# Differential scores: a copying minimum in place of a bare one, and an exponential on chip memory

## The chip, the core and the metric

The kernel runs on one NeuronCore of one Trainium2 chip. The core's engines run side by side, each through its own list of instructions in order: TensorE (PE; its weight loads are shown as PEld), VectorE (DVE), ScalarE (ACT), GpSimd (POOL) and SyncE (SP), which here only issues transfers. [...] The metric is the device time of one execution in microseconds (us); lower is better.

## What is computed

One layer of a bidirectional encoder over 1040 tokens (1024 plus 16 meta tokens) of width 1024: a SwiGLU block, a mixing block whose heads are split between differential attention and windowed attention, and a second SwiGLU block. The change lies in the differential attention, 4 heads with two score maps each:

```python
def attend(qb):
    s = jnp.einsum('bqhcd,bkhcd->bhcqk', qb, k, preferred_element_type=jnp.float32) * scale
    p = jax.nn.softmax(s, axis=-1)
    a = p[:, :, 0] - lam * p[:, :, 1]
    return jnp.einsum('bhqk,bkhe->bqhe', a.astype(v.dtype), v)
```

Each of the two maps c = 0, 1 of a head is a softmax over all 1040 keys; the second is weighted with a learned number and subtracted from the first, and the difference multiplies the values.

## The kernel before

The queries are handled in units of 128 rows, 8 units to a head, 32 in all; below, "unit 16" is the first one of the third head, and its two maps are 16a (c = 0) and 16b (c = 1). `scores` handles one map of one unit: six matmuls (three column ranges, with the keys split into a high and a low part) write the negated scores into a PSUM tile `ds` of 1040 columns, DVE reduces it to the row minimum `dmx`, and ACT takes the exponential out of PSUM into the SBUF tile `dp`, with the row sum as a second result. The tile `ds` spans three of the eight PSUM banks and there is one for each c (rings `ds0` and `ds1`, one slot each; the first three units use `ds0` for both), so the matmuls of the next unit's map must wait until the last reader of this one's `ds` is through. The two remaining banks are one slot `dt` for transposes and one slot `do` for products.

`combine` then makes the difference: DVE takes the reciprocals `drz` of the row sums (L797), POOL scales the second map (L799), DVE adds the first one to it (L800). Two units later PE transposes the result in three pieces through the slot `dt` (L1173 twice, L1181), each copied to `at` by ACT (L1178, L1182) or DVE (L1176), and every second unit the transposed rows multiply the values (L1189). Between these, PE works through products of the output projection with the windowed heads (L167 there). Loads of the next head's keys and queries pass through ACT (`kh` at L117, `qst` at L765) and POOL.

The tiles `dp` have three slots for each c, `dmx` two. The program is written as generators that take turns, but the framework's scheduler settles each engine's final order from its own timing model, over the whole program.

The window attention ahead of it already contains the instruction that the change uses, with a mask as its second input:

```python
nc.vector.tensor_tensor_reduce(
    out=p4[:, g, :w], in0=ps[:, :w], in1=mk[:, :w], scale=1.0,
    scalar=nsink[:, hh : hh + 1], op0=ALU.add, op1=ALU.min, accum_out=mx[:, g : g + 1],
)
```

Of the kernel before, what the change touches and what calls it, by code (L numbers as in the profile page):

```python
# [10 lines left out]
F32 = mybir.dt.float32  # L11
F32R = mybir.dt.float32r
AF = mybir.ActivationFunctionType
ALU = mybir.AluOpType
AX = mybir.AxisListType
# [3 lines left out]
P = 128  # L19
# [4 lines left out]
L = SEQ + NM  # L24
# [27 lines left out]
def layer(  # L52
# [4 lines left out]
    nc = tc.nc  # L57

    def mk_pool(name, bufs=1, side="left", space=None):
        kw = {"space": space} if space is not None else {}  # L60
        return tc.tile_pool(name=name, bufs=bufs, reuse_waits="tile", side=side, **kw)
# [21 lines left out]
    cpool = ctx.enter_context(mk_pool("cpool"))  # L83
# [9 lines left out]
    gains = const("gains", [P, 4, KT])  # L93
    eps = cpool.tile([P, 1], F32, name="eps")
    nc.vector.memset(eps, EPS)
    warm = cpool.tile([P, 1], F32, name="warm")
    nc.scalar.activation(warm, eps, AF.Abs_reciprocal_sqrt)
    nc.vector.tensor_scalar(gains, gains, -0.5 / D, None, op0=ALU.mult)
# [83 lines left out]
    def chunk_aps(ps, chunks):  # L182
        off = OFF if chunks is CH_ALL else 0
        return [ps[:, off + c0 : off + c0 + n] for c0, n in chunks], ps[
            :, off : off + chunks[-1][0] + chunks[-1][1]
        ]
# [592 lines left out]
    def scores(head, qt, c, tiles, ds):  # L779
        khs, kls, qs = head[:3]  # L780
        ps_p, z = tiles
        ps = ds.tile([P, 1536], F32, tag="ds", name="ds")
        outs, full = chunk_aps(ps, CH_ALL)
        for i, kk in enumerate((khs[c], kls[c])):
            for o, (c0, n) in zip(outs, CH_ALL):
                nc.tensor.matmul(
                    o, qs[c][:, qt * P : (qt + 1) * P], kk[:, c0 : c0 + n], start=i == 0, stop=i == 1
                )
        mx = dp.tile([P, 1], F32, tag=f"dmx{c}", name=f"dmx{c}")
        nc.vector.tensor_reduce(mx, full, axis=AX.X, op=ALU.min)  # L790
        p = dp.tile([P, L], F32, tag=f"dp{c}", name=f"dp{c}", bufs=3)
        nc.scalar.activation(p, full, AF.Exp, bias=mx, scale=-1.0, accum_out=z[:, c : c + 1])
        ps_p.append(p)

    def combine(ps_p, z):
# [9 lines left out]
    with ExitStack() as st:  # L805
# [236 lines left out]
        for i, (kv, n) in enumerate(units):  # L1042
            if i + 1 < len(units):
                keys[i + 1] = win_keys(*units[i + 1])
            p4 = win_scores(kv, n, [qs[kv, g] for g in range(4)], keys.pop(i))
            if prev:
                win_values(*prev)
            if i == 13:
                for _ in fill:
                    pass  # L1050
                st_u.close()
                kp = Rings(st_k, "kp", "right")
                for tag, bufs in (("v", 2), ("qst", 3), ("kh", 3), ("kl", 3), ("kraw", 1), ("qraw", 1)):
                    kp.reserve(tag, bufs)
                dp = Rings(st_k, "dp", "right", bufs=2)
                for tag, bufs in (("dp0", 3), ("dp1", 3), ("at", 2), ("oh", 2)):
                    dp.reserve(tag, bufs)
                ds0 = Rings(st_k, "ds0", "right", space=PSUM).reserve("ds")
                heads[0] = load_head(0)
            prev = (kv, n, p4)  # L1060
            if i in EARLY:
                for t in EARLY[i]:
                    sc[t] = score_tiles()
                    for c in range(2):
                        scores(heads[0], t, c, sc[t], ds0)
                    pend[t] = combine(*sc.pop(t))
            if n == NB - 1 and kv == 0:
                for g in range(4):
                    qs[1, g] = win_q(4 + g)
# [9 lines left out]
    with ExitStack() as st:  # L1079
        op = Rings(st, "op").reserve("ow_hi").reserve("ow_lo")  # L1080
# [123 lines left out]
        for i in range(NQ + 4):  # L1204
# [3 lines left out]
            def do_scores(c):  # L1208
                if N_EARLY <= i < NQ:
                    scores(heads[i // NB], i % NB, c, sc[i], ds1 if c else ds0)  # L1210
# [40 lines left out]
            if i >= 7 and (i - 7) % 4 == 0:  # L1251
                hd2, c = divmod((i - 7) // 4, 2)
# [168 lines left out]
```

## Time and profile before

| | |
|---|---|
| time, median of 3 runs | 2092.57 us (2092.17 to 2096.58) |
| profiled execution, its own time | 2091.47 us |
| its span, first to last instruction | 2089.7 us |
| PE busy | 1956.9 us (94%) |
| DVE busy | 1262.0 us (60%) |
| POOL busy | 993.3 us (48%) |
| ACT busy | 882.8 us (42%) |
| mean granted PE clock | 0.973 of full speed |

The busy times are shares of the whole span; what a stage can gain is read from the waits inside it. A busy PE is not PE at its peak, since matmuls overlap and their ends are modelled.

### The profile page before, as it was taken

The page shows a single profiled execution, that of the slowest core. Times are in us where ns is not written, and L with a number is a line of the kernel's source. Part 1 is how long each engine was busy: PE and PEld are TensorE (multiplying, and loading weights), DVE is VectorE, ACT ScalarE, POOL GpSimd, SP SyncE. Part 2 cuts the span into 40 slices and gives each one's busy share as a digit, 9 for nine tenths or more (in the row PEclk, how much of TensorE's full clock was granted, in tenths as well). Part 3 has the DMA queues.
Part 4 walks back from the last instruction along what each step waited for, and adds up shares of the span by engine and source line. Part 5 has one row for each costly group of instructions (what it writes and reads, how often), then busy time and mean ns, then how long its engine had stood idle before and what let it go on. Part 6 is the DMA issues. An engine that isn't in the chain of part 4 may idle for free. (4 is left out here: it accounts for less than half of the span.)

```text
span 2089.7 us, 30414 instructions
## 1 busy us (share of the span) xinstructions
PE 1956.9 (94%) x11508; PEld 1701.2 (81%) x11508; DVE 1262.0 (60%) x1843; ACT 882.8 (42%) x1611; POOL 993.3 (48%) x811
## 2 busy tenths in 40 slices
PE   6999999998999989899978898897999999989998
PEld 5999999998999879778756677675788888867877
DVE  6755555548874661276668677466655455487745
ACT  6433333334432431366566666353333333344433
POOL 0555554545443740576446442017754554454543
PEclk8999999999999999999979999998999999999999
DMA  4332322328422351544443321522333233385122
GB/s 157 110 118 97 117 91 99 108 94 314 153 62 81 130 165 62 152 118 121 109 102 91 83 75 53 194 92 81 122 106 111 86 106 112 116 297 166 61 81 81
DMA packets 106002, 244.14 MB, mean 117 GB/s; under 512 B 14208, under 2 KB 29008, under 8 KB 105856
## 3 DMA queue, kind: packets, MB, share of 16 engines
q1 hardware_dynamic: 94336, 204.53, 30.9%
q0 software_dynamic: 11520, 37.67, 4.6%
q8 instruction: 90, 1.47, 0.3%
q14 instruction: 56, 0.46, 0.1%
HBM read 169.86 MB, written 65.44 MB: 113 GB/s over the span
## 5 line engine op out<-in xcount | busy, mean ns | idle before, releaser
L226 PE MATMUL p<-t_hi,wch 128*128 128x260 f32 (+1 forms) x528 | 142.9, 325 | 9.4 <-DVE u L114 9.4
L226 PE MATMUL p<-b_hi,wah 128*128 128x260 f32 (+1 forms) x528 | 144.4, 328 | 7.0 <-ACT b_hi L117 3.8
L226 PE MATMUL p<-b_hi,wal 128*128 128x260 f32 (+1 forms) x528 | 142.3, 325 | 6.4 <-DVE wal L114 6.4
L226 PE MATMUL p<-b_lo,wah 128*128 128x260 f32 (+1 forms) x528 | 143.7, 325 | 0.0
L226 PE MATMUL p<-t_lo,wch 128*128 128x260 f32 (+1 forms) x528 | 142.2, 324 | 0.0
L226 PE MATMUL p<-t_hi,wcl 128*128 128x260 f32 (+1 forms) x528 | 141.9, 323 | 0.0
L114 DVE TENSOR_TENSOR u<-p,m 128x520 f32<-128x520 f32 (+1 forms) x88 | 61.0, 693 | 129.2 <-PE p L226 129.1
L114 POOL TENSOR_TENSOR ru<-rg,ru 128x512 f32<-128x512 f32 x44 | 87.6, 1990 | 106.8 <-DVE hb L149 74.0
L226 PE MATMUL p<-t_hi,wbh 128*128 128x260 f32 (+1 forms) x504 | 133.7, 321 | 2.6 <-ACT wbh L117 2.6
L226 PE MATMUL p<-t_lo,wbh 128*128 128x260 f32 (+1 forms) x504 | 135.9, 320 | 0.0
L226 PE MATMUL p<-t_hi,wbl 128*128 128x260 f32 (+1 forms) x504 | 133.3, 320 | 0.0
L117 ACT CAST wch<-ru 128x512 fp32r<-128x512 f32 x88 | 54.8, 623 | 183.8 <-issue 89.5
L574 PE MATMUL pA<-bh,wh 128*128 128x260 f32 (+1 forms) x432 | 116.3, 323 | 5.4 <-DVE h L581 5.4
L117 ACT CAST wbh<-s 128x512 fp32r<-128x512 f32 x84 | 52.3, 622 | 152.1 <-PE p L226 137.3
L574 PE MATMUL pA<-bl,wh 128*128 128x260 f32 (+1 forms) x432 | 115.5, 321 | 0.0
L114 POOL TENSOR_TENSOR s<-ru 128x512 f32<-128x512 f32 x42 | 57.4, 1368 | 120.3 <-DMA ru<-wu 60.9
L574 PE MATMUL pA<-bh,wl 128*128 128x260 f32 (+1 forms) x432 | 112.3, 319 | 0.0
L114 DVE TENSOR_TENSOR bl<-r,bh 128x520 fp32r<-128x520 f32 (+1 forms) x126 | 109.9, 907 | 2.3 <-ACT bh L117 2.0
L114 POOL TENSOR_TENSOR s<-wr 128x384 f32<-128x384 f32 x48 | 55.2, 1153 | 114.0 <-DVE wl L114 94.2
L117 ACT CAST wh<-s 128x384 fp32r<-128x384 f32 x96 | 49.1, 515 | 136.8 <-PE pA L574 66.6
L581 DVE SCALAR_TENSOR_TENSOR h<-pA,h 128x520 f32<-128x520 f32 (+1 forms) x96 | 66.2, 691 | 63.1 <-PE pA L574 63.0
L117 ACT CAST wah<-rg 128x512 fp32r<-128x512 f32 x88 | 54.4, 621 | 117.9 <-PE p L226 89.2
(289 smaller groups left out, 6128.0 us busy)
## 6 DMA issues: line engine op xcount, KB each, us to landing
rg<-wg SPq DMA_DIRECT2D x44, 512.0 KB, 3.6
ru<-wu SPq DMA_DIRECT2D x44, 512.0 KB, 5.2
wr<-wd SPq DMA_DIRECT2D x24, 768.0 KB, 4.4
r<-g_t SPq DMA_DIRECT2D x12, 780.0 KB, 5.9
r<-g_t SPq DMA_DIRECT2D x12, 768.0 KB, 5.8
g_b<-g POOLq DMA_DIRECT2D x27, 260.0 KB, 5.2
r<-g_b SPq DMA_DIRECT2D x9, 780.0 KB, 4.9
g_b<-g POOLq DMA_DIRECT2D x27, 256.0 KB, 5.5
```

The lines of the kernel that those rows point to most:

```text
L114: eng.tensor_tensor(out, a, b, op=op)
L117: nc.scalar.copy(hi, src)
L226: nc.tensor.matmul(o, w_k(ww, k), x[:, k, c0 : c0 + cn], start=first and k == 0 and i == 0, stop=k == hk - 1 and i == 2, skip_group_check= ...
L574: nc.tensor.matmul(o, w_k(ww, k), xx[:, c0 : c0 + cn], start=new and k == 0 and q == 0, stop=k == DNG - 1 and q == 2, skip_group_check=not ...
L581: nc.vector.scalar_tensor_tensor(hs, full, 0.5, hs, op0=ALU.mult, op1=ALU.add)
```

## The change

The row minimum is no longer a reduction that only reads. One DVE instruction adds zero to the scores, writes the sum (the scores themselves) to `dp` in SBUF, and leaves the row minimum in `dmx`; the zeros are a column `zero` of one element per partition, read with a stride of 0. The exponential then reads `dp` and writes `dp`. The slot of `dp` is taken by the DVE instruction now, not by ACT.

```diff
     nc.vector.memset(eps, EPS)
+    zero = cpool.tile([P, 1], F32, name="zero")
+    nc.vector.memset(zero, 0.0)
...
         mx = dp.tile([P, 1], F32, tag=f"dmx{c}", name=f"dmx{c}")
-        nc.vector.tensor_reduce(mx, full, axis=AX.X, op=ALU.min)
         p = dp.tile([P, L], F32, tag=f"dp{c}", name=f"dp{c}", bufs=3)
-        nc.scalar.activation(p, full, AF.Exp, bias=mx, scale=-1.0, accum_out=z[:, c : c + 1])
+        nc.vector.tensor_tensor_reduce(
+            out=p, in0=full, in1=zero.broadcast_to([P, L]), scale=1.0, scalar=3.4028234663852886e38,
+            op0=ALU.add, op1=ALU.min, accum_out=mx,
+        )
+        nc.scalar.activation(p, p, AF.Exp, bias=mx, scale=-1.0, accum_out=z[:, c : c + 1])
         ps_p.append(p)
```

The scheduler orders the whole program anew. Three places show what that does; a name in square brackets is the engine whose progress the instruction waits for (Pool is POOL, Activation is ACT, DMAHW a transfer), and line numbers of the changed kernel stand 2 to 5 higher. All three are at units 16 and 17, the first of the third head.

On DVE, before:

```order
L790 TENSOR_REDUCE dmx0_13802<-ds_13795 128x1 [waits PE_49]
L1176 COPY at_13674<-dt_13769 128x4x128 [waits PE_49]
L800 SCALAR_TENSOR_TENSOR dp0_13737<-dp0_13737,drz_13817,dp1_13748 128x1040 [waits Pool_49]
L790 TENSOR_REDUCE dmx1_13813<-ds_13806 128x1 [waits PE_49]
L1176 COPY at_13794<-dt_13821 128x4x128 [waits PE_49]
```

and in the changed kernel:

```order
L793 ISA dp1_13816,dmx1_13815<-ds_13808,zero_68 128x1040 [waits PE_49]
L793 ISA dmx1_13815 128x1
L1181 COPY at_13676<-dt_13771 128x4x128 [waits PE_49]
L805 SCALAR_TENSOR_TENSOR dp0_13738<-dp0_13738,drz_13819,dp1_13749 128x1040 [waits Pool_49]
L793 ISA dp1_13869,dmx1_13868<-ds_13861,zero_68 128x1040 [waits PE_49]
L793 ISA dmx1_13868 128x1
L793 ISA dp0_13805,dmx0_13804<-ds_13797,zero_68 128x1040 [waits PE_49]
L793 ISA dmx0_13804 128x1
```

Each reduction has become a pair, the pass over 1040 columns and a short one that stores the minimum; maps 16b and 17b (`ds_13808`, `ds_13861`) now stand ahead of 16a (`ds_13797`).

On PE, from the last matmul of map 16a (`ds_13795`) to the last transposition of unit 13 (`dt_13783`, out of `dp0_13618`, the tile whose slot 16a's `dp` gets), before:

```order
L786 MATMUL ds_13795<-kl_13582,qst_13583 128x264
L1173 MATMUL dt_13769<-ident_62,dp0_13618 128x128 [waits Activation_49]
L1173 MATMUL dt_13769<-ident_62,dp0_13618 128x128 x3
L1189 MATMUL do_13827<-at_13674,v_13034 128x256 [waits Activation_49]
L1189 MATMUL do_13827<-at_13674,v_13034 128x256 x3
L786 MATMUL ds_13806<-kh_13594,qst_13596 128x264 [waits Pool_49]
L786 MATMUL ds_13806<-kh_13594,qst_13596 128x512
L786 MATMUL ds_13806<-kh_13594,qst_13596 128x264
L786 MATMUL ds_13806<-kl_13595,qst_13596 128x264
L786 MATMUL ds_13806<-kl_13595,qst_13596 128x512
L786 MATMUL ds_13806<-kl_13595,qst_13596 128x264
L1181 MATMUL dt_13783<-ident_62,dp0_13618 16x128 [waits DVE_49]
```

and in the changed kernel, where 16a and 16b stand directly ahead of this piece:

```order
L1178 MATMUL dt_13771<-ident_62,dp0_13619 128x128 [waits Activation_49]
L1178 MATMUL dt_13771<-ident_62,dp0_13619 128x128 x3
L1194 MATMUL do_13829<-at_13676,v_13036 128x256 x4
L788 MATMUL ds_13861<-kh_13596,qst_13598 128x264 [waits DVE_49]
L788 MATMUL ds_13861<-kh_13596,qst_13598 128x512
L788 MATMUL ds_13861<-kh_13596,qst_13598 128x264
L788 MATMUL ds_13861<-kl_13597,qst_13598 128x264
L788 MATMUL ds_13861<-kl_13597,qst_13598 128x512
L788 MATMUL ds_13861<-kl_13597,qst_13598 128x264
L1186 MATMUL dt_13785<-ident_62,dp0_13619 16x128 [waits DVE_49]
```

Score matmuls wait for DVE in place of ACT, and map 17b (`ds_13861`) has moved up by a whole unit; the last transposition of unit 13 still stands behind the matmuls of 16a.

On ACT, where the second half of a head is loaded, before:

```order
L1182 COPY at_13674<-dt_13783 16x128 [waits PE_49]
L792 ACTIVATE dp0_13804,dz_13792<-ds_13795,dmx0_13802 128x1040 [waits DVE_49]
L765 CAST qst_14104<-qraw_14101 128x1024 [waits DMAHW6_49,DMAHW4_49]
L792 ACTIVATE dp1_13815,dz_13792<-ds_13806,dmx1_13813 128x1040 [waits DVE_49,Pool_49]
L1192 COPY oh_13233<-do_13827 128x256 [waits PE_49]
```

and in the changed kernel:

```order
L767 CAST qst_14106<-qraw_14103 128x1024 [waits DMAHW6_49,DMAHW5_49]
L797 ACTIVATE dp1_13816,dz_13794<-dp1_13816,dmx1_13815 128x1040 [waits DVE_49,Pool_49]
L1187 COPY at_13676<-dt_13785 16x128 [waits PE_49]
L797 ACTIVATE dp1_13869,dz_13849<-dp1_13869,dmx1_13868 128x1040 [waits DVE_49,Activation_49,Pool_49]
L797 ACTIVATE dp0_13805,dz_13794<-dp0_13805,dmx0_13804 128x1040 [waits DVE_49]
```

The copy out of the transposes' slot (L1182, now L1187) stood ahead of `qst`, which waits for a transfer; now it stands behind it and behind an exponential.

## Rows read from the trace of the kernel before

**Rows 1.** Busy time by stretch: us, then each engine's busy us, granted clock, DMA.

```profile
1045.00:1170.00 125.00, 99.36 (x469) 75.27 (x469) 87.59 (x99) 83.96 (x140) 68.31 (x45) 0.89 0.32 87
1170.00:1312.00 142.00, 130.56 (x687) 104.36 (x685) 98.97 (x118) 88.45 (x159) 53.09 (x35) 0.99 0.27 78
```

**Rows 2.** Waits of all engines, 1045 to 1312: who waited, total us, times, longest.

```profile
PEld ds L786 <- ACT dp L792: 27.6, 28, 3.1
...
PE ds L786 <- ACT dp L792: 17.9, 15, 2.9
...
PE dt L1173 <- ACT at L1182: 6.8, 11, 1.1
```

**Rows 3.** PE in time: waits of maps 1a,1b,4b,6b,7a,13b,17b,26b,30a: start, us, [idle before].

```profile
1063.97 0.74 PE L786 MATMUL ds<-kh,qst 128*128 128x264 f32 x3 [1.06 <-ACT dp L792]
...
1067.82 1.23 PE L786 MATMUL ds<-kh,qst 128*128 128x264 f32 x3 [2.64 <-ACT dp L792]
...
1076.38 1.23 PE L786 MATMUL ds<-kh,qst 128*128 128x264 f32 x3 [1.46 <-ACT dp L792]
...
1092.75 1.00 PE L786 MATMUL ds<-kh,qst 128*128 128x264 f32 x3 [2.86 <-ACT dp L792]
...
1107.05 1.24 PE L786 MATMUL ds<-kh,qst 128*128 128x264 f32 x3 [1.84 <-ACT dp L792]
...
1150.35 0.74 PE L786 MATMUL ds<-kh,qst 128*128 128x264 f32 x3 [1.44 <-ACT dp L792]
...
1194.22 0.74 PE L786 MATMUL ds<-kh,qst 128*128 128x264 f32 x3 [2.10 <-ACT dp L792]
...
1257.75 0.74 PE L786 MATMUL ds<-kh,qst 128*128 128x264 f32 x3 [0.80 <-ACT dp L792]
...
1289.60 0.74 PE L786 MATMUL ds<-kh,qst 128*128 128x264 f32 x3 [0.46 <-ACT dp L792]
```

**Rows 4.** DVE groups by line and shape: busy us, mean ns, idle before and releaser.

```profile
L790 DVE TENSOR_REDUCE dmx<-ds 128x1 f32<-128x1040 f32 x64 | 78.7, 1236 | 22.6 <-PE ds L786 22.2
L800 DVE SCALAR_TENSOR_TENSOR dp<-dp,drz,dp 128x1040 f32<-128x1040 f32 x32 | 45.4, 1420 | 3.6 <-POOL dp L799 3.2
...
L972 DVE CUSTOM_DVE_ANT_0 p<-ws,mask,nsink 128x400 f32<-128x400 f32 x48 | 29.4, 625 | 15.0 <-PE ws L968 10.2 <-PE wt L1012 4.4
...
L972 DVE CUSTOM_DVE_ANT_0 p<-ws,mask,nsink 128x272 f32<-128x272 f32 x16 | 7.8, 493 | 24.2 <-PE ws L968 22.8 <-PE wt L1012 1.4
...
L972 DVE DVE_READ_ACCUMULATOR2_ANT mx<- 128x1 f32 x64 | 5.1, 80 | 0.0
```

**Rows 5.** The same view for ACT.

```profile
L792 ACT ACTIVATE dp<-ds,dmx 128x1040 f32<-128x1040 f32 x64 | 71.8, 1121 | 20.4 <-DVE dmx L790 17.6 <-DVE drz L797 2.8
...
L988 ACT ACTIVATE p<-p,mx 128x400 f32<-128x400 f32 x48 | 30.2, 631 | 17.8 <-DVE mx L972 17.6
...
L988 ACT ACTIVATE p<-p,mx 128x272 f32<-128x272 f32 x16 | 8.3, 521 | 4.8 <-DVE mx L972 3.6 <-POOL p L996 1.2
...
L835 ACT ACTIVATE z<-pj 128x1040 f32<-128x1040 f32 x4 | 4.1, 1029 | 0.0
...
L117 ACT CAST kh<-kraw 128x1040 fp32r<-128x1040 f32 x7 | 7.4, 1058 | 5.3 <-DMA kraw<-ka_d 4.9 <-PE ds L786 0.4
```

**Rows 6.** Two DVE lines: duration ns minimum, median, maximum; first and last start.

```profile
L972 DVE CUSTOM_DVE_ANT_0 p<-ws,mask,nsink x64: 478/624/637, 859.3 to 1035.9; 128x400 f32<-128x400 f32 x48, 128x272 f32<-128x272 f32 x16
...
L800 DVE SCALAR_TENSOR_TENSOR dp<-dp,drz,dp x32: 1289/1294/3117, 1066.6 to 1303.7; 128x1040 f32<-128x1040 f32 x32
```

**Rows 7.** Reductions of L790 alone, in a stretch throughout which DVE was busy.

```profile
1098.00:1106.00 8.00, 2.54 (x3) 1.00 0.00 0
```

**Rows 8.** ACT in order of time, ahead of the wait of map 17b.

```profile
1188.37 0.25 ACT L1182 COPY at<-dt 16x128 f32<-16x128 f32 x1
...
1192.00 1.04 ACT L765 CAST qst<-qraw 128x1024 fp32r<-128x1024 f32 x1 [2.26 <-DMA qraw<-qa_d]
```

**Rows 9.** Busy time of a stretch with a low clock, columns as in rows 1.

```profile
1066.00:1078.00 12.00, 7.64 (x26) 6.22 (x27) 7.42 (x8) 7.78 (x14) 5.61 (x5) 0.50 0.42 103
```

## The prediction

> **What bounds the kernel now.** I read the page's busy shares first (PE 94%, the others far below), then the busy time by stretch, then the waits in the stage that the change touches, then PE's waits one by one, and last the durations of single operations. The shares say that PE sets the time nearly everywhere, so a change on DVE and ACT counts only as far as PE waits less or more. The 64 score maps run between 1045 and 1312 us. PE is busy there for 99.36 of 125 and 130.56 of 142 us [rows 1]: 37 us idle. The largest piece is 17.9 us, 15 times, in which the matmuls into `ds` waited for the exponential to leave that slot; the 27.6 us of the weight loads beside it lie partly under running matmuls and are not added [rows 2]. DVE is busy for 186.6 of the 267 us (70%), ACT for 172.4 (65%) [rows 1].
>
> Which maps waited tells more than the total. Six waits belong to maps of c = 1: 1b, 4b, 6b, 13b, 17b and 26b, 2.64 + 1.46 + 2.86 + 1.44 + 2.10 + 0.80 = 11.3 us. One is 1a, 1.06 us. The other eight are maps of c = 0 from 7a (1.84) to 30a (0.46), 17.9 - 11.3 - 1.1 = 5.5 us [rows 3].
>
> **The sum.** It is made against the profiled execution's own 2091.47 us, 1.1 below the median of the runs and inside reach of their lowest.
>
> **Where the slot comes free earlier.** Before, `ds` is held through the reduction (1236 ns), whatever ACT still has in its list, and the exponential (1121 ns) [rows 4, 5]. Now one DVE pass frees it. For c = 1 nothing else holds that pass back: the slot of `dp` it writes was last read by L800 of three units before, which stands ahead of it on DVE itself. So the waits of c = 1 should go, and with them 1a's, where three units share one `ds` and no old `dp` is in the way. One I do not count: 17b's. Its exponential stood behind `qst`, 2.26 us late from a transfer [rows 8]. In the new order 17b goes a unit earlier, but the transposes right behind it need a copy that now stands behind the same `qst`; before, that copy was done at 1188.6 us, ahead of it [rows 8]. That wait changes its name and stays. Gain: 11.3 - 2.1 + 1.1 = 10.3 us.
>
> **Where it does not.** For c = 0 the slot of `dp` is freed by the last transposition of three units before, and in the pieces of PE's order shown with the change that transposition stands behind the scores of the unit that wants the slot. Before, only the exponential had to wait for it; the reduction did not. Now the pass itself stands until then, and `ds` stays full. So PE's order from that transposition to the next c = 0 scores must now cover the pass in place of the exponential: 1285 + 80 ns (next part) against 1121, +0.25 us. I leave the eight waits as they are and add this to each: 8 x 0.25 = +2.0 us. Bounds: -5.5, if DVE is ready sooner than ACT was, and the price in the last rival.
>
> **The DVE pass is longer.** The same instruction ran in the window attention, out of PSUM with a second input from SBUF: 625 ns for 400 columns, 493 for 272 [rows 4], 1.03 ns a column. For 1040 columns that gives 625 + 640 x 1.03 = 1285 ns, and the stored minimum costs 80 more [rows 4]: +129 ns on 1236, 8.3 us for 64. DVE's 80 us of idle time in the stage cover that except where it never paused. In the 8 us of one such stretch stood three reductions [rows 7], 0.4 us; I count twice that: +0.8. Bounds: 0, and 8.3 if all of it lay on the path. POOL works on SBUF beside it. The old instruction of this kind, with one input from SBUF, kept a narrow spread (624 ns median, 637 at most), while L800, with both inputs there, went from 1294 ns median to 3117 [rows 6]. I take the first as the model. [...]
>
> **The exponential reads SBUF.** For the source alone the trace has a pair: 1029 ns for 1040 columns out of PSUM, 1058 out of SBUF, +29. The in-place exponential of the window attention, 631 ns for 400 and 521 for 272 columns, extends to 631 + 640 x 0.86 = 1181 for 1040, +60 on today's 1121 [rows 5]. I take the 60, since it is the same function in place: 3.8 us of ACT for 64, under 95 us of idle time; three that meet a busy ACT make +0.2. Bounds: 0 and 3.8. [...]
>
> **Nothing else on the path.** The memset of `zero` lies beside the first loads, and no transfer is added. The scheduler also shuffles matmuls of the second SwiGLU block; no row prices that, and I count 0.
>
> Sum: 2091.47 - 10.3 + 2.0 + 0.8 + 0.2 = 2084.2; I say 2084.
>
> **The rivals.**
>
> *All waits go, and low clock with them.* [...] For it: the clock is 0.89 over the first part, where most idle time lies, and 0.99 over the second [rows 1]. Against: the slot of `dp` for c = 0. Time: 2091.5 - 17.9 - 3.8 + 1.0 = 2071.
>
> *The waits move to the transposes.* PE passes the scores earlier and stands at `dt`, one slot, copied out by an ACT whose own list is no shorter. For it: 17b's place, and 6.8 us of such waits today [rows 2]. Against: 1b, 4b and 6b lie in the part where few transposes are due. Then the 10.3 us come back, and the time is 2094.5; half of them, 2089.
>
> *The slot of `dp` takes the slot of `ds` along* (slower). If every c = 0 map from the fourth unit on waited as today's eight do on the mean, 5.5 / 8 = 0.69 us, and the 0.25 on top, that would be 28 x 0.94 = 26.3 us where 5.5 stand now: 2091.5 + 20.8 - 10.3 + 1.0 = 2103. It decides from where the mean passes (10.3 + 5.5 - 1.0) / 28 = 0.53 us a unit. For it: the transposition stands behind the scores at this place in both orders. Against: the trace shows no exponential that waited for such a transposition, which had the same rule.
>
> **How the numbers follow.** The forecast, gains of 4 to 14 us: 0.47. All waits and clock, 14 to 24: 0.20. Waits move: 0.20, of which 0.18 lie within 0.2% of the median (4.2 us, about what a measurement of this kernel can tell from no change) and 0.02 above. The slot of `dp`: 0.13, of which 0.02 lie within and 0.11 above. So faster 0.67, same 0.20, slower 0.13. The range that leaves out no more than 2 in 10 reaches from 2071 (the second case) to 2094 (the third).
>
> **What would show it.** In the changed profile no score matmul waits for ACT; in its place stand waits for DVE of 6 to 9 us, nearly all of c = 0. The pass takes 1.27 to 1.30 us plus 0.08, the exponential 1.14 to 1.19. PE's idle time from 1045 us to the last scores falls from 37 to about 30 us. The prediction is wrong if waits for copies into `at` grow by more than 6 us, if the pass is above 1.5 us, if DVE stands long at the pass for a transposition, or if the second SwiGLU block changes its length by more than 3 us.

## The result and the profile after

The changed kernel took 2109.15 us (median, 2104.73 to 2111.4), the kernel before 2092.37 us beside it: a ratio of 1.008, 95% interval 1.006 to 1.0097. It is slower by about 17 us where 2084 was forecast. Its profiled execution, the fastest of its runs, took 2104.73 us (before: 2091.47), with a span of 2103.0 us, so the traces show 13.3 of the 17 us.

Busy time of the changed kernel by stretch, columns as in [rows 1]; the first two lines answer to [rows 1], the third to [rows 9], and the last three split up the end of the stage:

```profile
1045.00:1170.00 125.00, 100.57 (x481) 77.12 (x482) 90.89 (x133) 85.37 (x141) 70.82 (x45) 0.90 0.33 90
1170.00:1312.00 142.00, 124.67 (x642) 98.78 (x640) 93.21 (x145) 90.20 (x155) 52.84 (x34) 0.97 0.23 69
...
1066.00:1078.00 12.00, 9.23 (x54) 7.12 (x55) 11.40 (x19) 10.13 (x18) 7.49 (x7) 1.00 0.41 129
...
1210.00:1250.00 40.00, 34.68 (x185) 27.36 (x184) 29.25 (x44) 26.99 (x46) 17.76 (x11) 1.00 0.23 73
1250.00:1290.00 40.00, 37.07 (x180) 29.44 (x179) 25.95 (x41) 24.12 (x42) 9.53 (x7) 0.91 0.11 33
1290.00:1334.00 44.00, 35.92 (x166) 26.93 (x166) 19.44 (x31) 19.22 (x35) 7.43 (x6) 0.92 0.32 102
```

The first stretch is a little better than before: the twelve microseconds that had a clock of 0.50 [rows 9] now have 1.00. The second is worse: PE is busy for 124.67 us instead of 130.56, at 0.97 instead of 0.99. From the first score to the first product behind the stage (`po`) it is 286.1 us, before 275.6. Of these 10.5 us, 5.7 are busy time (242.3 against 236.6 us of PE for the same matmuls, clock 0.93 against 0.95) and 4.8 are idle time. From 1045 to 1312 us PE stands idle for 41.8 us, where 37 stood before and about 30 were forecast.

PE's waits in the changed kernel, 1045 to 1312 us, columns as in [rows 2]:

```profile
PE dt L1178 <- ACT at L1187: 13.5, 14, 2.3
PE dt L1178 <- ACT at L1183: 11.1, 7, 4.1
...
PE ds L788 <- POOL qst L768: 4.0, 1, 4.0
PE dt L1186 <- ACT at L1183: 3.2, 4, 1.1
PE ds L788 <- DVE dmx L793: 3.0, 5, 1.3
```

The waits of the scores are gone as planned: 17.9 us before [rows 2], now 3.0 for DVE (6 to 9 were forecast), and one of 4.0 for a late load. But PE now stands at `dt`, the one slot of the transposes, until ACT has copied it out: 13.5 + 11.1 + 3.2 = 27.8 us. Before, the largest such row was 6.8 [rows 2], and with the other two, in the same stretch, it was 9.9 us:

```profile
PE dt L1173 <- ACT at L1178: 1.7, 1, 1.7
...
PE dt L1181 <- ACT at L1178: 1.4, 2, 0.7
```

The operations themselves, by line (columns as in [rows 4]):

```profile
L793 DVE CUSTOM_DVE_ANT_0 dp<-ds,zero 128x1040 f32<-128x1040 f32 x64 | 78.2, 1237 | 23.5 <-PE dt L1186 12.8 <-PE ds L788 7.2 <-ACT oh L1197 2.3
...
L793 DVE DVE_READ_ACCUMULATOR2_ANT dmx<- 128x1 f32 x64 | 5.3, 82 | 0.0
...
L797 ACT ACTIVATE dp<-dp,dmx 128x1040 f32<-128x1040 f32 x64 | 74.4, 1162 | 23.5 <-DVE dmx L793 19.6 <-DVE drz L802 3.4
```

The pass takes 1237 + 82 ns, the reduction took 1236; the exponential 1162 ns, before 1121 [rows 4, 5]. Passes stood 12.8 us for a transposition (`PE dt L1186`): that is the slot of `dp0`.

One place shows the whole chain. In order of time, DVE, then ACT, then PE of the changed kernel (start us, us, operation, [idle before <- releaser]):

```profile
1305.90 1.24 DVE L793 CUSTOM_DVE_ANT_0 dp<-ds,zero 128x1040 f32<-128x1040 f32 x1 [0.70 <-PE dt L1186]
...
1305.90 0.25 ACT L1187 COPY at<-dt 16x128 f32<-16x128 f32 x1 [0.37 <-PE dt L1186]
1306.17 1.28 ACT L1108 ACT_TABLE_LOAD   x1
1307.46 0.69 ACT L1108 ACTIVATE nr<-do,eps 128x512 f32<-128x512 f32 x1
1308.17 1.28 ACT L797 ACT_TABLE_LOAD   x1
1309.46 1.16 ACT L797 ACTIVATE dp<-dp,dmx 128x1040 f32<-128x1040 f32 x1
...
1310.62 0.56 ACT L1183 COPY at<-dt 128x512 f32<-128x512 f32 x1
...
1311.24 1.12 PE L1178 MATMUL dt<-ident,dp 128*128 128x128 f32 x4 [4.08 <-ACT at L1183]
```

The pass starts when the transposition has given back its `dp` slot. The exponential behind it has been put after the reciprocal square root of a head norm, with a table load ahead of each; the copy out of `dt` stands behind all four, and PE waits 4.08 us. ACT is busy all that time, so here it is the order of its list that holds the copy, not a late pass. At the end of the stage before, exponential and copy stood ahead of that norm:

```profile
1300.71 1.11 ACT L792 ACTIVATE dp<-ds,dmx 128x1040 f32<-128x1040 f32 x1
...
1301.83 0.56 ACT L1178 COPY at<-dt 128x512 f32<-128x512 f32 x1
1302.40 1.28 ACT L1103 ACT_TABLE_LOAD   x1
1303.70 0.69 ACT L1103 ACTIVATE nr<-do,eps 128x512 f32<-128x512 f32 x1
```

A second place of this kind, at 1153.82 us, cost 3.65 us. From 1040 to 1340 us the new order has 13 table loads of 1.28 us where the old one has 11.

### The profile page after: what moved, and what is told of

Read it like the earlier page. It is cut to its first block, busy times and chain, and to the rows that moved or that the text cites. A ratio compares the mean times of both kernels' runs of the same rounds, so it can differ in the third digit from the quotient of the medians.

```text
span 2103.0 us, 30481 instructions
## 1 busy us (share of the span) xinstructions
PE 1961.2 (93%) x11508; PEld 1702.6 (81%) x11508; DVE 1282.6 (61%) x1908; ACT 887.8 (42%) x1613; POOL 980.7 (47%) x811
## 5 line engine op out<-in xcount | busy, mean ns | idle before, releaser
L116 POOL TENSOR_TENSOR ru<-rg,ru 128x512 f32<-128x512 f32 x44 | 66.9, 1521 | 105.4 <-DVE hb L151 72.4
L116 POOL TENSOR_TENSOR s<-rg,s 128x512 f32<-128x512 f32 x44 | 67.7, 1539 | 97.6 <-ACT u L365 75.6
```

The costliest lines, as they stand in the source:

```text
L116: eng.tensor_tensor(out, a, b, op=op)
```

## The experiments

Four explanations were held against each other. PASS: DVE's longer instruction costs. SLOT: the pass of c = 0 has to wait for the slot of `dp0`. ORDER: the scheduler's new order costs, not the change. DEPEND: the change costs through its waits, in any order. The kernel before was measured beside every one of them, at 2089.9 to 2092.5 us, and each ratio is to that.

**One half each, order free.** e1 makes the pass only for c = 1, which has no slot of `dp` to wait for, e2 only for c = 0:

```diff
+        if c == 1:            # e2: c == 0
             nc.vector.tensor_tensor_reduce(out=p, ...)
             nc.scalar.activation(p, p, AF.Exp, ...)
+        else:
+            nc.vector.tensor_reduce(mx, full, axis=AX.X, op=ALU.min)
+            nc.scalar.activation(p, full, AF.Exp, ...)
```

> The copying pass for the maps of c = 1 only; c = 0 keeps the bare reduction and the exponential out of PSUM. Theory SLOT (the pass for c = 0 must stand until the transposition of three units before has freed its slot of dp, DVE stands with it, and the order that the scheduler has to build around this delays the transposes): no slot is in the way for c = 1, so its waits of 11.3 us go and nothing comes in their place: 2080 to 2088 us. Theory ORDER (the scheduler's new order alone, with c = 1 ahead and ACT's copies out of dt behind exponentials and loads, is what costs): still above before, 2094 to 2102. Theory PASS (the longer DVE pass and the exponential out of SBUF cost by themselves): half of the loss, about 2100.

> The copying pass for the maps of c = 0 only. SLOT: the whole loss or more, since the gain on c = 1 is missing, 2105 to 2120 us, with DVE standing for the transposition L1186 for 10 us or more. ORDER: between before and the change, 2095 to 2105. PASS: half of the loss, about 2100.

e1: 2113.25 us, 1.0109 (1.009 to 1.0127). e2: 2112.28, 1.0111 (1.0088 to 1.0134). Each half alone costs as much as both together, or more; and e1 has no pass that waits for `dp0`, so SLOT alone cannot be it. In e2 DVE stands at the pass for the transposition for 2.3 us, where SLOT expected 10 or more.

**A fourth slot, order free**, in the changed kernel (e3) and in the one before (e4). To make room, `hrm`, a tile of the output projection, gives one of its two slots up:

```diff
-                for tag, bufs in (("dp0", 3), ("dp1", 3), ("at", 2), ("oh", 2)):
+                for tag, bufs in (("dp0", 4), ("dp1", 3), ("at", 2), ("oh", 2)):
...
-            ht = op.tile([P, 512], F32, tag="hrm", name="hrm", bufs=2)
+            ht = op.tile([P, 512], F32, tag="hrm", name="hrm", bufs=1)
```

> The change with a fourth slot of dp for c = 0; to make room in SBUF the tile hrm of the output projection has one slot in place of two, which the next kernel has as well. SLOT: DVE no longer stands for the transposition of three units before, waits of PE for ACT's copies out of dt fall back to some 12 us, and the time is 8 to 18 us below that of the next kernel. ORDER: waits at dt stay near 29 us and the time is 10 us or more above the next kernel. PASS: 8 to 16 us above it.

> The kernel before with a fourth slot of dp for c = 0 and one slot of hrm: what both of these do without the change. The trace of before shows no exponential that waited for a transposition, so the fourth slot should give nothing, and one slot of hrm may cost a few us: 2090 to 2098 us in all theories.

e3: 2113.2 us, 1.0108 (1.0094 to 1.0123). e4: 2100.48, 1.0047 (1.0033 to 1.006). The slot given back does not bring the time back (in an order of its own, e3 still has 7.6 us of DVE at the pass for a transposition), and even the kernel before loses 10 us when its buffers, and with them its order, are another.

**The order held.** From here on, edges without waits (issue order only) fix each engine's instructions in the order of another kernel, by their place in the order of writing:

```diff
         layer(tc, io)
+        hold_order(tc, nc)
...
+        places = [k for first, n in runs for k in range(first, first + n)]
+        for x, y in zip(places, places[1:]):
+            tc.add_manual_dep(written[y], written[x].name, issue, reason="held order")
```

e5 is the whole change, e6 is e1, both in the order of before. In e5 DVE is left free; with the same four engines held and its old buffers, the kernel before comes out in its old order on DVE too; in e5 it does not. e7 and e8 price the pass alone: it writes back into PSUM, so that no buffer changes hands differently, with the order free (e7) and held (e8).

```diff
-            out=p, in0=full, in1=zero.broadcast_to([P, L]), ...
+            out=full, in0=full, in1=zero.broadcast_to([P, L]), ...
...
-        nc.scalar.activation(p, p, AF.Exp, ...)
+        nc.scalar.activation(p, full, AF.Exp, ...)
```

> The whole change, with the instructions of PE, ACT, POOL and SP in the very order of the kernel before; DVE alone is free, since with three slots of dp0 its old order could not run. ORDER (the loss is that of the new order, and the change itself gains a little): 2083 to 2093 us, ratio 0.995 to 1.001; PE's waits at ds for ACT go from 17.9 to under 5 us, and its waits at dt stay near the 12 us of before. DEPEND (the change itself makes the copies out of dt late, in any order): 2103 to 2112 us, waits at dt of 25 us or more.

> The copying pass for c=1 alone, as in e1_copy_c1, with all five engines in the order of the kernel before. ORDER: 2083 to 2091 us (e1 in an order of its own took 2113), waits of PE at ds for ACT halved. DEPEND: 2105 us or more, as e1.

> The pass writes its copy back onto the scores in PSUM, and the exponential reads PSUM as before: buffers and waits are those of before, DVE's instruction alone is another, and the order is free. ORDER: a new order costs, 2097 to 2113 us. DEPEND: nothing that matters has changed, 2090 to 2096 us. PASS (DVE's pass is the cost): 2100 us or more, here and in e8.

> e7 with all five engines in the order of the kernel before: the price of the pass on DVE and of nothing else. ORDER and DEPEND: 2090 to 2095 us. PASS: 2100 us or more.

e5: 2121.67 us, 1.0131 (1.0118 to 1.0144). e6: 2091.53, 0.9996 (0.9984 to 1.0009). e7: 2092.04, 0.9997 (0.9986 to 1.0009). e8: 2093.64, 1.0009 (0.9996 to 1.0022). PASS falls: the instruction costs nothing that can be told from 0 (at most 0.0022 in e8), though written back to PSUM it takes 1246 + 138 ns, more than in the changed kernel. e6 against e1 is the same kernel in two orders: 22 us, so for c = 1 it is ORDER. But ORDER does not cover c = 0: e5 is slow with PE, ACT, POOL and SP in the old order, so c = 0 has a cost of its own. e7 does not bear on ORDER: left free, its order in this stage came out as before but for a few weight pieces of the output projection. So it is the new holding of `ds` and `dp`, not the longer instruction, for which the scheduler orders the stage anew. The shorter waits of e6 (10.6 us at `ds` for ACT) brought no time that can be measured.

**What c = 0 costs, and whether the order alone costs.** e9 is e5 with four slots of `dp0` and two of `dp1`, e10 its control without the change, e11 is e2 with PE, ACT, POOL and SP held as in e5. e12 is the kernel before, untouched, with ACT, DVE, POOL and SP in e1's order.

> e5 with a fourth slot for dp0, taken from dp1 (four and two slots): the whole change, PE, ACT, POOL and SP in the order of the kernel before, DVE free. SLOT (in that order the pass of c=0 waits for a slot of dp0, and nothing else is lost): 2083 to 2096 us, where e5 took 2121.7; PE's waits at ds under 8 us. If the loss at held order has another cause: 2110 us or more.

> The kernel before with four slots of dp0 and two of dp1, PE, ACT, POOL and SP in its old order, DVE free: what e9 is to be held against. All theories: 2090 to 2097 us; above 2100 the two slots of dp1 cost by themselves, and e9 is read against this run.

> The copying pass for c=0 alone, three slots of dp0, PE, ACT, POOL and SP in the order of the kernel before, DVE free. SLOT: all of e5's loss is c=0's, 2112 to 2125 us. If the loss of e5 needs both halves: about 2100 us.

> The kernel before, nothing of the change in it, with ACT, DVE, POOL and SP in the order that e1_copy_c1 ran in, PE's order left to the scheduler. ORDER: the loss of e1 comes with its order, 2103 to 2115 us. DEPEND (the loss needs the new buffers): 2090 to 2096 us.

e9: 2143.42 us, 1.0248 (1.0228 to 1.0269). e10: 2134.23, 1.0202 (1.0184 to 1.0221). With two slots of `dp1` the control itself is 42 us slow (in it ACT stood 43.7 us for L800, which gives those slots back), so the pair decides nothing. e11: 2124.39, 1.016 (1.0131 to 1.0189): all of e5's loss is c = 0's. e12: 2120.17, 1.014 (1.0117 to 1.0162): no line of the change is in it, and it loses 28 us. An order by itself can cost as much as this. It is not e1's loss over again, though: the largest of PE's waits in e12, 1040 to 1370 us, is that for the exponential at `ds`, which e1 has to a smaller part (13.8 us):

```profile
PE ds L786 <- ACT dp L792: 23.9, 20, 2.6
PE dt L1173 <- ACT at L1182: 12.5, 14, 5.3
PE dt L1181 <- DVE at L1176: 9.9, 9, 2.0
```

**The slot, with a control that holds.** e13 and e14 take the slots of e3 and e4 and hold PE, ACT and POOL in the old order. e15 holds only PE of e1, e16 all but PE.

> The whole change with four slots of dp0 and three of dp1 (hrm gives one up), PE, ACT and POOL in the order of the kernel before, DVE and SP free. SLOT (c=0's half costs because, in that order, its pass has to wait for the slot that the transposition of three units before gives back): 2083 to 2098 us, within 6 us of e14, and E(c=0) no longer stands 40 us and more in wait for the pass. If c=0's half costs for another reason than the slot: 2115 us or more, as e5 (2121.7).

> The kernel before with the slots of e13 and PE, ACT and POOL in its old order: what e13 is held against. 2090 to 2100 us under either; above 2105 the one slot of hrm or the freed order of SP costs by itself.

> The copying pass for c=1 alone with PE in the order of the kernel before and the other four engines free. If PE's order is what costs e1 its 21 us: 2088 to 2095 us, as e6. If the order of the copies and exponentials on ACT and DVE costs: 2100 us or more.

> The counterpart: ACT, DVE, POOL and SP in the order of the kernel before, PE free. If PE's order is what costs: 2100 us or more. If the others' order costs: 2088 to 2097 us.

e13: 2091.94 us, 1.0008 (0.9997 to 1.0019). e14: 2096.46, 1.0023 (1.0013 to 1.0032). e5 and e13 differ by the fourth slot: 30 us. (They differ in `hrm` and in the order of SP as well, but with both of these e14 is 5 us slower than before, not faster.) ACT's wait for the pass, the first of its rows from 1040 to 1370 us, in e5:

```profile
ACT dp L797 <- DVE dmx L793: 55.8, 32, 4.6
```

and in e13:

```profile
ACT dp L797 <- DVE dmx L793: 19.9, 12, 4.6
```

With three slots the pass is late for 32 exponentials, with four for 12, near the 17.6 us of before [rows 5]. Here SLOT is shown, and with it DEPEND for c = 0. How the 30 us come about is shown in part only: in e5 no more than 6.6 us of DVE's idle time at the pass end with the transposition, and the rest was not followed; DVE's order is new in e5 and nearly the old one in e13. e15: 2092.19 us, 0.9999 (0.9989 to 1.001); e16: 2090.88, 0.9996 (0.9985 to 1.0007). Holding either side keeps the old time. In e15 the engines left free come out nearly in their old order, so it is much the same kernel as e6; in e16 PE has a new order and loses nothing. So not every new order costs, and which engine's order carries the loss of e1 stays open.

**The order of the changed kernel itself.** e17 is e13 with PE, ACT and POOL in the order of the changed kernel; e18 is the kernel before with ACT, DVE, POOL and SP in that order.

> e13 (the whole change, four slots of dp0) with PE, ACT and POOL in the order that the changed kernel itself ran in, in place of the order of the kernel before; DVE and SP free. If the 17 us of the changed kernel are the price of its order, with no slot in want any more: 2103 to 2115 us. If they are still the slot of dp0: 2088 to 2097 us, as e13.

> The kernel before, nothing of the change in it, with ACT, DVE, POOL and SP in the order of the changed kernel, PE left to the scheduler. ORDER: 2103 us or more. If that order is bad only together with the new buffers: 2090 to 2097 us.

e17: 2119.26 us, 1.0122 (1.0101 to 1.0143). e18: 2130.3, 1.0175 (1.0151 to 1.0198). Busy time from the first score to `po`, columns as in [rows 1], in e14, e13 and e17:

```profile
1049.90:1324.70 274.80, 236.33 (x1188) 185.28 (x1186) 185.39 (x218) 173.59 (x303) 118.17 (x77) 0.95 0.29 85
```

```profile
1050.80:1317.90 267.10, 232.51 (x1188) 180.31 (x1186) 188.97 (x282) 175.54 (x303) 117.79 (x77) 0.97 0.30 88
```

```profile
1050.40:1352.20 301.80, 248.21 (x1188) 193.76 (x1186) 196.31 (x282) 178.50 (x305) 119.02 (x79) 0.91 0.27 79
```

The same 1188 matmuls, with the same slots, take 267.1 us in one order and 301.8 in the other: 15.7 us of the difference is busy time at a lower clock (0.91 against 0.97), 19.0 is idle time. PE's waits in e13 and e17, 1040 to 1350 us:

```profile
PE dt L1178 <- ACT at L1187: 9.1, 13, 1.5
PE dt L1186 <- ACT at L1183: 6.1, 4, 2.8
...
PE ds L788 <- DVE dmx L793: 3.7, 4, 1.9
PE dt L1178 <- ACT at L1183: 3.2, 2, 2.5
```

```profile
PE dt L1178 <- ACT at L1183: 16.1, 9, 4.1
PE dt L1178 <- ACT at L1187: 14.8, 15, 2.6
PE dt L1186 <- ACT at L1183: 7.7, 5, 4.8
...
PE ds L788 <- DVE dmx L793: 2.5, 4, 1.5
```

Waits at `dt` for ACT go from 18.4 to 38.6 us, those at `ds` stay small. So the order that came with the change costs 27 us with the slot conflict taken away (DVE stands 0.2 us for the transposition in e17). e3 and e13 say the same of e3's order: one program in two orders, 21 us apart. The 38 us of e18 are not the price of that order in the changed kernel. PE's largest wait there, 1040 to 1365 us, is one that the changed kernel no longer has:

```profile
PE ds L786 <- ACT dp L792: 29.4, 18, 4.3
PE dt L1173 <- ACT at L1178: 12.1, 11, 4.4
```

The whole change in the old order on all five engines was not tried: with three slots the first pass of such a unit would stand on DVE ahead of a copy that its own slot waits for. No version measured here beats the kernel before.

## Why the prediction was wrong

**The step that failed** is what the new order was priced at. The prediction put 0 on reordering, for the second SwiGLU block, and did not price it in the stage of the scores at all but for 17b. The block kept its length, 463.7 against 462.8 us from its first matmul into `p` to the first into `pA`. The stage did not. The rival *the waits move to the transposes* named the place, but capped the loss at the 10.3 us gained; e17 lost 27 us to e13. The copies out of `dt` came to stand behind exponentials and table loads, and the lower clock (0.93 against 0.95) put about as much on top: 5.7 us of busy time beside 4.8 us of idle time. Two of the signs of being wrong came true: waits for copies into `at` grew from 9.9 to 27.8 us, and DVE stood 12.8 us at the pass for a transposition.

**The slot of `dp`.** The rival on it had the mechanism right for the old order: 20.8 us of loss was its estimate for c = 0, and e11 lost 32. The forecast's +2.0 for the same thing was wrong in kind: it took the waits of eight units and left the others at none, but in e5 the pass is late for 32 exponentials. It also took the old order of DVE for granted, which cannot run with three slots. In the changed kernel the scheduler evaded part of the wait (ACT stands 19.6 us for the pass, in e5 55.8) by an order that costs by itself. How much of its 17 us is one and how much the other stays open: no run separates the two with three slots.

**The gain.** Where neither cost is in the way the mechanism holds: e13's stage is 7.7 us shorter than e14's, and the sum's terms for the stage were -10.3 + 2.0 + 0.8 + 0.2 = -7.3. That the two are so close is luck: the +2.0 is for the conflict that the fourth slot takes away, and 3.8 of the 7.7 us are busy time at a higher clock (0.97 against 0.95), which the sum did not count. The waits at `ds` went from 16.7 us in e14 to 3.7 in e13, more than forecast, but those at `dt` for ACT rose from 13.8 to 18.4 even in the old order: the rival of the waits that move was right about a third of the gain. By the ratios of e13 and e14 about 3 us (0.0015) of it reach the end, and their intervals overlap; in the profiled executions 5.2 us go again in the second down projection (below). For c = 1 alone the gain is 3.0 us in the stage of e6's profile (272.6 against 275.6) and nothing in its median.

**The small terms.** The pass was to take 1285 + 80 ns and took 1237 + 82; +0.8 was counted, and e8, which carries a pass somewhat longer than this and nothing else, is 0.0009 above before with an interval that holds 0. The exponential was to take 1181 ns and took 1162, +41 on before. The pass kept a narrow spread, as the instruction taken for its model had [rows 6]: it stayed within 1219 to 1242 ns. L805 went to 3471, and that longest one, at 1103.5 us, ran beside two POOL operations, on `kl` (2.44 us) and `qst` (3.24 us).

```profile
L793 DVE CUSTOM_DVE_ANT_0 dp<-ds,zero x64: 1219/1241/1242, 1049.2 to 1305.9; 128x1040 f32<-128x1040 f32 x64
...
L805 DVE SCALAR_TENSOR_TENSOR dp<-dp,drz,dp x32: 1286/1301/3471, 1066.9 to 1313.0; 128x1040 f32<-128x1040 f32 x32
```

**The clock.** Here the rival *all waits go, and low clock with them* was right in a part: 1066 to 1078 us rose from 0.50 to 1.00. No run shows the 3.8 us that its sum takes off for that: the three matmuls of a map with `kh` took 1.23 us at 0.50 (before, at 1072.62 us) and 0.74 us at 1.00 (changed, at 1072.54 us), 0.60 of the time, and by that the 7.64 us of [rows 9] would lose about 3.1, an estimate. Elsewhere the clock fell: it was 0.52 for some 7 us each from about 1283 and from about 1310 us on. In the 7 us ahead of each fall PE was busy for 4.70 and for 3.48 us, and waits at `dt` of 2.30 and 4.08 us end there:

```profile
1276.00:1283.00 7.00, 4.70 (x26) 3.79 (x25) 3.56 (x6) 6.94 (x10) 1.21 (x1) 0.99 0.16 49
1283.00:1290.00 7.00, 7.00 (x20) 5.20 (x20) 4.26 (x7) 3.09 (x6) 3.40 (x2) 0.52 0.00 0
1303.00:1310.00 7.00, 3.48 (x18) 2.19 (x16) 3.22 (x4) 5.25 (x7) 1.26 (x1) 1.00 0.35 112
1310.00:1317.00 7.00, 5.62 (x15) 4.21 (x16) 3.31 (x5) 2.19 (x6) 2.47 (x2) 0.52 0.22 72
```

The kernel before, in the same part of the stage:

```profile
1250.00:1290.00 40.00, 36.98 (x202) 29.91 (x201) 31.06 (x37) 27.17 (x50) 11.35 (x8) 1.00 0.11 35
1290.00:1334.00 44.00, 38.79 (x179) 28.55 (x179) 18.46 (x26) 17.32 (x33) 7.47 (x6) 1.00 0.47 151
```

## What to carry to other kernels

Where a scheduler sets the order, a change in how long a buffer is held is two changes: price the waits, and then read the new order for what now stands ahead of the copies out of a single-slot buffer; a list of waits that go away is no bound on those that come. Hold the old order and try again before blaming the instruction: 22 us of e1, 21 of e3 and all 28 of e12 were order. And an earlier first write into a ring needs its slot earlier: count for each ring what gives its slot back, and whether that stands behind the instruction that now wants it.

## Not expected of the hardware

DVE's pass out of PSUM with a second output to SBUF is as fast as the reduction that writes one column (1237 against 1236 ns), and 82 ns to store the minimum come on top. Written back to PSUM it takes 1246 + 138 ns (e8).

The second down projection, whose work no kernel here changes, took 183.3 to 184.1 us in five of the six profiled kernels without `zero` (185.7 in e12) and 185.5 to 188.5 us in the fourteen with it. Its order differs a little in five of them, but two of these, e4 and e18, took 183.8 and 183.7 us. Its matmuls are longer. The clock was 0.99 in the kernel before and 0.98 in the changed one, but seven of the fourteen have 0.99 too and take 185.5 to 187.3 us. The costliest line of it in the kernel before and in the changed one:

```profile
L574 PE MATMUL pA<-bh,wh 128*128 128x512 f32 x144 | 57.0, 396 | 3.8 <-DVE h L581 3.8
```

```profile
L576 PE MATMUL pA<-bh,wh 128*128 128x512 f32 x144 | 57.9, 402 | 2.7 <-DVE h L583 2.7
```

The tile `zero` stands among the constants; whether it is the cause was not tried, and stays open. The longer projection is about 4 of the 13.3 us between the two profiled executions. e7 and e8 have the tile as well, and their times show no loss, 2092.04 and 2093.64 us.
